# FFN output product: six of eleven pairs of feature tiles by seven products, in two passes over the columns

## The chip, the cores and the metric

The kernel runs on one core of a Trainium2 chip. The metric is the device time of one execution, in microseconds (us). TensorE (PE) multiplies 128x128 tiles: a weight load (PEld) puts the standing operand in place, and a matmul moves the other operand past it into a bank of PSUM. VectorE (DVE), ScalarE (ACT) and GpSimd (POOL) work on SBUF and PSUM, each through its own queue in order. SyncE (SP) issues most of the transfers.

## The reference, cut to what matters

One decoder layer for 512 tokens of width 1024: two mixers on a normalised input, an output projection, and a SwiGLU feed-forward part (FFN), each with a norm before and behind and a residual. The change touches the last product, the norm behind it and the residual:

```
def swiglu(hn, w_ffn_in, w_ffn_out):          # w_ffn_out: 2816 x 1024
    a, b = jnp.split(hn @ w_ffn_in, 2, axis=-1)
    return (jax.nn.silu(a) * b) @ w_ffn_out
...
    ff = swiglu(rmsnorm(h, norm_ffn_pre[l]), w_ffn_in[l], w_ffn_out[l])
    h = h + rmsnorm(ff, norm_ffn_post[l])
```

All inputs and the output are float32.

## The kernel before

Every product in float32 is made of three matmuls on operands split in two: `split` (L103) copies a tile to a high part (float32r) on ACT and has DVE subtract it from its source for the low part (`lo_of`, L100). High by high, high by low and low by high are summed in PSUM. So each operand costs one ACT copy and one DVE subtraction, both inputs of which lie in SBUF when the source does.

Many products go by Strassen's and Winograd's scheme: an operand is cut in four quarters, seven products of quarters and of their sums (`PRODUCTS`, L213: a for weights, s for their sums, b for tokens, t for theirs) take the place of eight. The sums of weights are made on POOL (L230, L258), the results are put together by DVE from PSUM (`seven`, L263).

The FFN's first product (L1268 to L1283) takes eleven pairs f2 of feature tiles. Each loads 256 columns for the gate and for the other half (`feat_quarters`, L221), runs `feat_seven` (L287) twice, seven products of 12 matmuls with 256 columns each, and leaves silu(a) * b in `gt` (L1283), which holds for each pair four quarters: two feature tiles by two halves of the tokens.

The second product, up to the end, is the stage in question. `rows` (L1300) loads two feature tiles of `w_ffn_out` (each 128 x 1024), splits them into `wh` and `wl`, and splits the gate tiles into `gh` and `gl` (`gate_split`, L1264). `product(i, c, f)` (L1314) makes three matmuls of 512 columns for token tile i, column half c and feature tile f, with the gate as the standing operand. Eight banks of PSUM hold all of the result (4 token tiles x 2 halves). The first 18 feature tiles go one after the other over all eight banks. The last four go bank by bank (L1330), so that a token tile is finished while others still run: sum of squares on ACT (L1337), gain on DVE (L1342), power on POOL (L1341), scaling and residual on DVE (L1346), output on SP's or ACT's queue (L1347).

What sets the order: raw weights come by SP's queue into a ring of four buffers (`wraw`, L80), split ones lie in a ring of five (`wun`, L81), each released when its reader is done. Within an engine a planner orders the instructions by a simulated timeline (L1387); where `pinned` is set (L1329) the matmuls stay in the program's order. Buffers of a pool that is closed are taken over by the next pool when their last readers are done.

Of the kernel before, what the change touches and what calls it, by code (L numbers as in the profile page):

```python
# [10 lines left out]
F32 = mybir.dt.float32  # L11
# [5 lines left out]
P = 128  # L17
# [17 lines left out]
def hybrid_block(  # L35
# [1224 lines left out]
    NPF, REST = NF // 2, 4  # L1260
    gt = gp.tile([P, NPF, 4, H], F32, name="gt")
    gs = {}

    def gate_split(f):  # L1264
        gs[f] = [gp.tile([P, T], F32R, tag=n, name=n, bufs=REST + 2) for n in ("gh", "gl")]
        split(*gs[f], gt[:, f // 2, 2 * (f % 2) : 2 * (f % 2) + 2, :].rearrange("p t n -> p (t n)"))

    with tc.tile_pool(name="s7", bufs=2, side=RS, reuse_waits="tile") as s7:  # L1268
        for f2 in range(NPF):
# [13 lines left out]
            nc.vector.tensor_tensor(gt[:, f2], qb, qa, op=ALU.mult)  # L1283
    s6c.close()
    ps_ac.close()
    ps_c = ctx.enter_context(tc.tile_pool(name="ps_c", bufs=4, space=PSUM))


    def bank_c():
        return ps_c.tile([P, 512], F32, tag="c", name="pc")  # L1290

    with tc.tile_pool(name="s8", bufs=2, side=RS, reuse_waits="tile") as s8:
        gfin = s8.tile([P, D], F32, name="gfin", bufs=1)
        nc.scalar.dma_start(gfin, g_ffn_post.to_broadcast([P, D]))
        banks = [(f(), f()) for f in (bank_p, bank_b, bank_c, bank_c)]

        def col(name):
            return s8.tile([P, 1], F32, tag=name, name=name, bufs=NT)

        def rows(f2):  # L1300

            raws = [raw_of(w_ffn_out[f * P : (f + 1) * P, :]) for f in (2 * f2, 2 * f2 + 1)]
            res = []
            for e in range(2):
                gate_split(2 * f2 + e)
                wh = wun.tile([P, D], F32R, tag="wh", name="wh")
                wl = wun.tile([P, D], F32R, tag="wl", name="wl")
                split(wh, wl, raws[e][:, 0, :])
                res.append((wh, wl))
            return res  # L1310

        ws = {}

        def product(i, c, f):  # L1314
            ts_, cs, dst = slice(i * P, (i + 1) * P), slice(512 * c, 512 * (c + 1)), banks[i][c]
            (wh, wl), (gh, gl) = ws[f], gs[f]
            mm(dst, gh[:, ts_], wh[:, cs], start=(f == 0), stop=False)
            mm(dst, gh[:, ts_], wl[:, cs], start=False, stop=False)
            mm(dst, gl[:, ts_], wh[:, cs], start=False, stop=(f == NF - 1))

        for f2 in range(NPF):
            ws[2 * f2], ws[2 * f2 + 1] = rows(f2)
            for f in (2 * f2, 2 * f2 + 1):
                if f < NF - REST:
                    for i in range(NT):
                        for c in range(2):
# [64 lines left out]
```

## Time and profile before

| | |
|---|---|
| median of three runs | 1178.73 us (1178.39 to 1178.78) |
| profiled execution | 1178.72 us, its span 1176.9 us |
| PE busy | 1164.9 us, 99% |
| DVE busy | 844.0 us, 72% |
| ACT busy | 532.1 us, 45% |
| POOL busy | 333.5 us, 28% |
| granted clock of TensorE | 0.999 |

The span runs from the first to the last instruction. Busy is the time in which an engine executes something, including time in which an instruction that has begun is held up. A row of a group reads: line, engine, operation, output <- inputs, shape, count, busy time, mean of one in ns, and the idle time before them with what ended it.

### The profile page before, as it was taken

How to read it: one execution, taken by the hardware profiler on the slowest of the kernel's cores; microseconds unless marked ns; L12 is line 12 of the kernel's file. 1: busy time of each engine (PE TensorE's matmuls, PEld its weight loads, DVE VectorE, ACT ScalarE, POOL GpSimd, SP SyncE). 2: the span in 40 equal slices, each digit the busy share in tenths (PEclk: the TensorE clock that was granted, in tenths of full speed). 3: DMA queues.
4: the chain of work that ended last, by engine and by line, in shares of the span. 5: the costliest groups of instructions: out<-in, count | busy, mean ns of one | idle time of the engine just before them, and what ended most of it. 6: DMA issues, size and time to landing. Idle time of an engine off the chain costs nothing.

```text
span 1176.9 us, 18856 instructions
## 1 busy us (share of the span) xinstructions
PE 1164.9 (99%) x7529; PEld 1056.3 (90%) x7529; DVE 844.0 (72%) x1120; ACT 532.1 (45%) x899; POOL 333.5 (28%) x358
## 2 busy tenths in 40 slices
PE   9999999999999999999999999999999999999997
PEld 7988999988899998998899898888999999998886
DVE  7488888888577873786586567767799998773333
ACT  6476666666233434434243334335455444442321
POOL 2021112126644403320240200001356676610000
PEclk9999999999999999999999999999999999999999
DMA  7332122222641323115122434344033333353311
GB/s 235 99 99 74 62 72 64 77 77 92 194 148 60 93 90 114 55 53 154 36 82 82 133 90 134 126 160 126 19 108 108 109 108 108 108 162 101 97 36 72
DMA packets 146536, 118.25 MB, mean 100 GB/s; under 512 B 3832, under 2 KB 135168, under 8 KB 146448
## 3 DMA queue, kind: packets, MB, share of 16 engines
q1 hardware_dynamic: 145856, 115.85, 32.5%
q8 instruction: 59, 0.97, 0.4%
q10 hardware_dynamic: 592, 1.20, 0.3%
q14 instruction: 29, 0.24, 0.1%
HBM read 109.96 MB, written 7.08 MB: 99 GB/s over the span
## 4 chain that ended last, share of the span: by engine, by line
PE 92%; DVE 5%; issue 1%; ACT 1%; DMA 0%; POOL 0%; POOLq 0%; DVEq 0%; ACTq 0%
PE pp L95 41%; PE pb L95 20%; PE pa L95 20%; PE pc L95 5%; PE px L95 3%; PE pb L98 3%; DVE wl L101 1%; DVE sm L603 1%; ACT wh L104 1%; DVE sl L101 0%; DMA ysb<-in_x_dram 0%; DVE al L101 0%; DVE kl L101 0%; DVE qb L101 0%; DVE qa L101 0%
## 5 line engine op out<-in xcount | busy, mean ns | idle before, releaser
L101 DVE TENSOR_TENSOR wl<-raw,wh 128x1024 fp32r<-128x1024 f32 x196 | 260.7, 1338 | 60.3 <-ACT wh L104 59.3
L104 ACT ACTIVATE wh<-raw 128x1024 fp32r<-128x1024 f32 x194 | 195.2, 1014 | 203.4 <-PE pa L95 59.5
L95 PE MATMUL pp<-hT,wh 128*128 128x512 f32 (+1 forms) x304 | 112.0, 369 | 0.0
L95 PE MATMUL pp<-hL,wh 128*128 128x512 f32 (+1 forms) x304 | 107.7, 354 | 0.0
L95 PE MATMUL pp<-hT,wl 128*128 128x512 f32 (+1 forms) x304 | 107.6, 354 | 0.0
L258 POOL TENSOR_TENSOR st<-raw 128x512 f32<-128x512 f32 x28 | 44.4, 1608 | 170.3 <-DMA raw<-in_w_in_dram 170.3
L101 DVE TENSOR_TENSOR wl<-st,wh 128x1024 fp32r<-128x1024 f32 x54 | 75.1, 1392 | 13.1 <-ACT wh L104 12.1
L95 PE MATMUL pp<-qk,wh 128*128 128x512 f32 x256 | 80.1, 394 | 0.0
L230 POOL TENSOR_TENSOR st<-raw 128x512 f32<-128x512 f32 x40 | 61.1, 1528 | 50.3 <-DVE wl L101 50.3
L95 PE MATMUL pp<-wh,hT 128*128 128x256 f32 (+1 forms) x240 | 73.9, 309 | 0.1
L95 PE MATMUL pp<-wl,hT 128*128 128x256 f32 (+1 forms) x240 | 73.0, 305 | 0.7 <-DVE wl L101 0.4
L95 PE MATMUL pp<-wh,hL 128*128 128x256 f32 (+1 forms) x240 | 73.0, 305 | 0.2 <-DVE hL L101 0.2
L104 ACT ACTIVATE wh<-st 128x1024 fp32r<-128x1024 f32 x54 | 56.6, 1056 | 35.6 <-PE pp L95 15.6
L95 PE MATMUL pa<-hL,wh 128*128 128x264 f32 (+1 forms) x208 | 66.2, 318 | 0.0
L95 PE MATMUL pa<-hT,wh 128*128 128x264 f32 (+1 forms) x208 | 66.2, 318 | 0.0
L95 PE MATMUL pa<-hT,wl 128*128 128x264 f32 (+1 forms) x208 | 66.1, 318 | 0.0
L603 DVE TENSOR_TENSOR_SCAN sm<-sm,mask 128x528 f32<-128x528 f32 (+1 forms) x64 | 54.8, 857 | 14.3 <-ACT sm L600 13.5
L95 PEld LDWEIGHTS pp<-hT,wl 128*128 128x128 f32 x304 | 57.2, 188 | 8.4
L613 POOL CAST mg<-sp 128x32 fp32r<-128x32 f32 x32 | 7.5, 233 | 197.6 <-DVE sp L604 153.7
L95 PEld LDWEIGHTS pp<-hT,wh 128*128 128x128 f32 x304 | 57.3, 188 | 5.8
L95 PEld LDWEIGHTS pp<-hL,wh 128*128 128x128 f32 x304 | 57.4, 189 | 5.3
L95 PEld LDWEIGHTS pp<-qk,wh 128*128 128x128 f32 x256 | 47.7, 188 | 10.7
(346 smaller groups left out, 3680.3 us busy)
## 6 DMA issues: line engine op xcount, KB each, us to landing
raw<-in_w_in_dram SPq DMA_DIRECT2D x88, 512.0 KB, 4.2
raw<-in_w_ffn_in_dram SPq DMA_DIRECT2D x44, 512.0 KB, 3.8
raw<-in_w_ffn_out_dram SPq DMA_DIRECT2D x22, 512.0 KB, 3.6
raw<-in_w_ret_out_dram SPq DMA_DIRECT2D x16, 512.0 KB, 3.4
raw<-in_w_sb_out_dram SPq DMA_DIRECT2D x8, 512.0 KB, 3.9
raw<-in_w_out_dram SPq DMA_DIRECT2D x8, 512.0 KB, 4.0
ysb<-in_x_dram SPq DMA_DIRECT2D x4, 512.0 KB, 7.1
gb_d<-go SPq DMA_DIRECT2D x8, 256.0 KB, 2.0
```

The source lines that it names most:

```text
L95: return keep(nc.tensor.matmul(*args, **kw))
L98: return keep(nc.tensor.transpose(dst, src, idn))
L101: return nc.vector.tensor_tensor(lo, src, hi.bitcast(F32), op=ALU.subtract)
L104: ins = nc.scalar.activation(hi, src, AF.Copy)
L230: ins = nc.gpsimd.tensor_tensor(d, p, q, op=op)
L258: nc.gpsimd.tensor_tensor(d[:, k : k + 2], p[:, k : k + 2], q[:, k : k + 2], op=op)
L603: nc.vector.tensor_tensor_scan(rev, rev, mask[:, r0:][:, ::-1], 0.0, op0=ALU.mult, op1=ALU.max)
L613: nc.gpsimd.tensor_copy(g[:, two, 0:NM], m)
```

## The change

The stage now runs in two passes g over the columns (512 each), and a step takes a pair f2 of feature tiles (256 features) with the 512 columns and all 512 tokens. Pairs with an even number go by seven products of quarters (42 matmuls of 256 columns), those with an odd number by plain products (24 of 512 columns). `prepare(n)` loads the weights of step n, has POOL make the sums of weights and tokens, and splits all. Split operands lie in four rooms of 16 KB, two of which are the buffers `th` and `tl` of the stage before. The second pass takes the pairs from 10 down; the first four find their operands still in the rooms and prepare only weights. Seven products and the plain ones share eight banks (`new_banks`; plain products go to the banks of a12 with a22, and of s4 with x22, a quarter of its own). `combine` puts them together at the end of each pass, in SBUF (`ys`). The first two steps are prepared within the stage before. The steps 19 (pair 1, plain), 20 and 21 (pairs 2 and 0) of the second pass are interleaved product by product, so that token tiles 2 and 3 are finished behind s4 and 0 and 1 behind the last product. The norm's gain of the first pass runs during the second; the gains of tiles 2 and 3 in the second, and one residual sum for tiles 0, 2 and 3, go to POOL.

```diff
@@ -1257,13 +1257,55 @@
     gp = ctx.enter_context(tc.tile_pool(name="gp", bufs=1, side=LS, reuse_waits="tile"))
-    NPF, REST = NF // 2, 4
+    NPF, REST = NF // 2, 2
     gt = gp.tile([P, NPF, 4, H], F32, name="gt")
-    gs = {}
-
-    def gate_split(f):
-        gs[f] = [gp.tile([P, T], F32R, tag=n, name=n, bufs=REST + 2) for n in ("gh", "gl")]
-        split(*gs[f], gt[:, f // 2, 2 * (f % 2) : 2 * (f % 2) + 2, :].rearrange("p t n -> p (t n)"))
+    ops, ws = {}, {}
+    plain = lambda f2: f2 % 2 == 1
+    def pair_of(n):
+        return n if n < NPF else (10, 9, 8, 7, 6, 5, 4, 3, 1, 2, 0)[n - NPF]
+    rooms4 = [(gp, "go"), (tn, "th"), (tn, "tl")]
+    def prepare(n, sums):
+        g, f2 = n // NPF, pair_of(n)
+        raw = raw_of(w_ffn_out[2 * P * f2 : 2 * P * (f2 + 1), 512 * g : 512 * (g + 1)])
+        A11, A21 = raw[:, 0, 0:256], raw[:, 0, 256:512]
+        A12, A22 = raw[:, 1, 0:256], raw[:, 1, 256:512]
+        seven_, kept = not plain(f2), g == 1 and f2 >= NPF - 4
+        if seven_:
+            w = sums.tile([P, 4, H], F32, tag="st", name="st")[:, 0:3, :]
+            S2, S3, S4 = w[:, 0, :], w[:, 1, :], w[:, 2, :]
+            todo = [(gt[:, f2, 1, :], gt[:, f2, 1, :], gt[:, f2, 0, :], ALU.subtract)] if g == 0 else []
+            todo += [(S3, A11, A21, ALU.subtract), (A21, A21, A22, ALU.add), (S2, A21, A11, ALU.subtract), (S4, A12, S2, ALU.subtract)]
+            if not kept:
+                t = sums.tile([P, 4, H], F32, tag="st", name="st")[:, 0:3, :]
+                T2, T3, T4 = t[:, 0, :], t[:, 1, :], t[:, 2, :]
+                B11, T1, B21, B22 = [gt[:, f2, q, :] for q in range(4)]
+                todo += [(T2, B22, T1, ALU.subtract), (T3, T2, B11, ALU.subtract), (T4, B21, T2, ALU.subtract)]
+            for d, p, q, op in todo:
+                nc.gpsimd.tensor_tensor(d, p, q, op=op)
+        wh, wl = wun_split(raw.rearrange("p k (c n) -> p (k c) n", c=2))
+        ws[n] = {k: (wh[:, v], wl[:, v]) for k, v in dict(a11=0, s1=1, a12=2, a22=3).items()}
+        ws[n]["rows"] = [[v[:, 2 * k : 2 * k + 2].rearrange("p c n -> p (c n)") for v in (wh, wl)] for k in range(2)]
+        if kept:
+            ops[n] = ops[pair_of(n)]
+        else:
+            place, name = rooms4[pair_of(n) % 4]
+            if g:
+                place, name = rooms4[(2, 1, 0, 3)[(n - NPF) % 4]]
+            o = place.tile([P, 4, KH, H], F32R, name=name, bufs=1).rearrange("p a b n -> p (a b) n")
+            split(o[:, 0:4], o[:, 8:12], gt[:, f2])
+            ops[n] = {k: (o[:, v], o[:, 8 + v]) for k, v in dict(b11=0, t1=1, b12=1, b21=2, b22=3, t2=4, t3=5, t4=6).items()}
+        if seven_:
+            wh, wl = wun_split(w)
+            ws[n].update({k: (wh[:, v], wl[:, v]) for k, v in dict(s2=0, s3=1, s4=2).items()})
+            if not kept:
+                split(o[:, 4:7], o[:, 12:15], t)
     with tc.tile_pool(name="s7", bufs=2, side=RS, reuse_waits="tile") as s7:
         for f2 in range(NPF):
@@ -1281,70 +1323,175 @@
             nc.scalar.activation(qa, qa, AF.Silu)
             feat_seven(ub_, ntok, qb)
             nc.vector.tensor_tensor(gt[:, f2], qb, qa, op=ALU.mult)
+        for n in range(2):
+            prepare(n, sst)
     s6c.close()
-    ps_ac.close()
-    ps_c = ctx.enter_context(tc.tile_pool(name="ps_c", bufs=4, space=PSUM))
-
-
-    def bank_c():
-        return ps_c.tile([P, 512], F32, tag="c", name="pc")
     with tc.tile_pool(name="s8", bufs=2, side=RS, reuse_waits="tile") as s8:
         gfin = s8.tile([P, D], F32, name="gfin", bufs=1)
         nc.scalar.dma_start(gfin, g_ffn_post.to_broadcast([P, D]))
-        banks = [(f(), f()) for f in (bank_p, bank_b, bank_c, bank_c)]
-
...
-                            product(i, c, f)
+        rooms4.append((s8, "o4"))
+        sc = [[s8.tile([P, 1], F32, tag=f"sc{i}{c}", name="sc", bufs=1) for c in range(2 + 2 * (i < 2))] for i in range(NT)]
+        ys = [s8.tile([P, 4, 512], F32, name="y", bufs=2) for _ in range(2)]
+        names = ["a11", "s2", "s1", "s3", "s4", "a12", "a22"]
+        pairs = dict(PRODUCTS)
+        both_of, single, banks, keys, begun = {}, {}, {}, {}, set()
+        def new_banks():
+            begun.clear()
+            for a, room in zip(names, (bank_p, bank_p, bank_b, bank_b)):
+                v = room()
+                banks[a], keys[a], single[a] = [v[:, 0:256], v[:, 256:512]], [a, a], v
+            for t, two in enumerate((("a12", "a22"), ("s4", "x22"))):
+                both_of[t] = bank_a()
+                for c, a in enumerate(two):
+                    banks[a], keys[a] = [both_of[t][:, s, 256 * c : 256 * (c + 1)] for s in range(2)], [(t, 0), (t, 1)]
+            both_of["a12"], both_of["a22"] = [both_of[0][:, :, 256 * c : 256 * (c + 1)] for c in range(2)]
+            both_of["s4"], both_of["x22"] = [both_of[1][:, :, 256 * c : 256 * (c + 1)] for c in range(2)]
+        def three(d, key, x, w):
+            mm(d, x[0], w[0], start=key not in begun, stop=False, skip_group_check=True)
+            begun.add(key)
+            mm(d, x[0], w[1], start=False, stop=False, skip_group_check=True)
+            mm(d, x[1], w[0], start=False, stop=True, skip_group_check=True)
+        def tile_of(n, b, s):
+            return [v[:, P * s : P * (s + 1)] for v in ops[n][b]]
+        def product(n, a, parts=(0, 1)):
+            for s in parts:
+                three(banks[a][s], keys[a][s], tile_of(n, pairs[a], s), ws[n][a])
+        def plain_products(n, tokens_=(0, 1)):
+            for t in tokens_:
+                for s in range(2):
+                    for k in range(2):
+                        three(both_of[t][:, s, :], (t, s), tile_of(n, f"b{k + 1}{t + 1}", s), ws[n]["rows"][k])
+        def step(n):
+            if plain(pair_of(n)):
+                plain_products(n)
+            else:
+                for a in names:
+                    product(n, a)
+        def add(d, p, q):
+            nc.vector.tensor_tensor(d, p, q, op=ALU.add)
+        def whole(a):
+            return single[a].rearrange("p (s n) -> p s n", s=2)
+        def combine(y, a):
+            q11, q21, q12, q22 = [y[:, q, :].rearrange("p (s n) -> p s n", s=2) for q in range(4)]
+            p = both_of[a] if a in both_of else whole(a)
+            if a == "x22":
+                nc.scalar.activation(q22, p, AF.Copy)
+            elif a == "a11":
+                nc.scalar.activation(q11, p, AF.Copy)
+            elif a == "s2":
+                add(q21, p, q11)
+            elif a == "s1":
+                add(q12, p, q21)
+                add(q22, q12, q22)
+            elif a == "s3":
+                add(q22, p, q22)
+                add(q21, p, q21)
+            elif a == "s4":
+                add(q12, p, q12)
+            elif a == "a12":
+                add(q11, p, q11)
+            else:
+                add(q21, p, q21)
+        def columns(y, i, g, cn):
+            n0, n1, s = cn.start, cn.stop, i % 2
+            return y[:, 2 * (i // 2) + n0 : 2 * (i // 2) + n1, 256 * s : 256 * (s + 1)], gfin[:, 512 * g + 256 * n0 : 512 * g + 256 * n1].rearrange("p (c n) -> p c n", n=256)
+        def squares(i, g, cn, dst):
+            v, _ = columns(ys[g], i, g, cn)
+            sq = s8.tile([P, 2, 256], F32, tag="sq", name="sq")[:, : cn.stop - cn.start, :]
+            nc.scalar.activation(sq, v, AF.Square, scale=D**-0.5, accum_out=dst)
+        def scaled(i, g, cn):
+            v, w = columns(ys[g], i, g, cn)
+            (nc.gpsimd if g and i > 1 else nc.vector).tensor_tensor(v, v, w, op=ALU.mult)
+        both = slice(0, 2)
+        def finish(i, n):
+            rs = s8.tile([P, 1], F32, tag="rs", name="rs", bufs=NT)
+            nc.vector.scalar_tensor_tensor(rs, sc[i][0], 1e-6, sc[i][n - 1], op0=ALU.add, op1=ALU.add)
+            nc.gpsimd.tensor_tensor(rs, rs, nhalf, op=ALU.pow)
+            for g in range(2):
+                v, _ = columns(ys[g], i, g, both)
+                cs = slice(512 * g, 512 * (g + 1))
+                h = h2[:, i, cs].rearrange("p (c n) -> p c n", c=2)
+                if g or i == 1:
+                    nc.vector.scalar_tensor_tensor(v, v, rs, h, op0=ALU.mult, op1=ALU.add)
+                else:
+                    nc.scalar.activation(v, v, AF.Copy, scale=rs)
+                    nc.gpsimd.tensor_tensor(v, v, h, op=ALU.add)
+                queue = nc.scalar if i == 1 and g else nc.sync
+                queue.dma_start(out[i * P : (i + 1) * P, cs].rearrange("p (c n) -> p c n", c=2), v)
+        order = ["x22"] + names
+        new_banks()
+        last = 2 * NPF - REST - 1
+        for n in range(last):
+            if n >= 2:
+                prepare(n, s8)
+            if n == NPF:
+                for a in order:
+                    combine(ys[0], a)
+                new_banks()
+            if NPF + 2 <= n < NPF + 2 + NT:
+                squares(n - NPF - 2, 0, both, sc[n - NPF - 2][0])
+                scaled(n - NPF - 2, 0, both)
+            step(n)
+        for n in range(last, 2 * NPF):
+            prepare(n, s8)
         pinned[0] = True
-        for i in range(NT):
-            sc, fo = [col("sc0"), col("sc1")], s8.tile([P, D], F32, tag="fo", name="fo")
...
-                queue.dma_start(out[i * P : (i + 1) * P, cs], fo[:, cs])
+        plain_products(last, (1,))
+        for a in names:
+            if a == "a22":
+                plain_products(last, (0,))
+                combine(ys[1], "a12")
+                combine(ys[1], "a22")
+            for parts in ((0, 1),) if a != "a22" else ((0,), (1,)):
+                if a == "a22":
+                    i = parts[0]
+                    banks[a][i], keys[a][i] = bank_p()[:, 0:256], ("last", i)
+                for n in range(last + 1, 2 * NPF):
+                    product(n, a, parts)
+                if a == "a22":
+                    cs = slice(256 * i, 256 * (i + 1))
+                    add(ys[1][:, 1, cs], banks[a][i], ys[1][:, 1, cs])
+                    if i == 0:
+                        for e in range(2):
+                            squares(e, 1, slice(0, 1), sc[e][1])
+                            scaled(e, 1, slice(0, 1))
+                            nc.gpsimd.tensor_tensor(sc[e][0], sc[e][0], sc[e][1], op=ALU.add)
+                    squares(i, 1, slice(1, 2), sc[i][2])
+                    scaled(i, 1, slice(1, 2))
+                    finish(i, 3)
+            if a == "a11":
+                combine(ys[1], "x22")
+            if a[0] == "s" or a == "a11":
+                combine(ys[1], a)
+            if a == "s4":
+                for i in (2, 3):
+                    squares(i, 1, both, sc[i][1])
+                    scaled(i, 1, both)
+                for i in (2, 3):
+                    finish(i, 2)
 # ---- launch: one core; inputs and outputs as the reference has them ----
```

More of the change, by code (lines that the diff above doesn't have):

```diff
@@ L1312, in hybrid_block @@
[L1312 to L1324, printed above, removed]
-                    for i in range(NT):
-                        for c in range(2):
-                            product(i, c, f)
```

27 lines of the change are left out of this document (removed).

## The prediction

> **What bounds the kernel now.** I read the page's span and engine shares first, then the table of stretches for the last 200 us, then the chain of waits, and last the single instructions at the places that the change touches.
>
> ```profile
> span 1176.9 us, 18856 instructions
> PE 1164.9 (99%) x7529; PEld 1056.3 (90%) x7529; DVE 844.0 (72%) x1120; ACT 532.1 (45%) x899; POOL 333.5 (28%) x358
> ```
>
> ```profile
> 972.00:1012.00 40.00, 40.00 (x338) 40.00 (x337) 33.30 (x35) 18.47 (x22) 26.28 (x17) 1.00 0.36 106
> 1041.00:1051.00 10.00, 10.00 (x86) 10.00 (x85) 6.31 (x8) 5.45 (x6) 0.00 (x0) 1.00 0.61 178
> 1051.00:1111.00 60.00, 60.00 (x267) 49.65 (x266) 22.96 (x24) 17.16 (x22) 0.00 (x0) 1.00 0.37 120
> 1111.00:1150.00 39.00, 39.00 (x174) 32.30 (x173) 12.74 (x13) 10.28 (x13) 0.00 (x0) 1.00 0.13 41
> ```
>
> The columns of the second are the stretch, its length, busy time and count of PE, PEld, DVE, ACT and POOL, the granted clock, and the DMA. PE has no idle time from 972 to 1150 and runs at full clock; in the stage to be changed (from 1051 on) DVE is busy 38% and less, and POOL not at all. So time leaves this stage only with matmul time, and DVE and POOL have room for additions, unless these get in each other's way. The chain of waits gives the pitch of matmuls (start, length, count):
>
> ```profile
> 1038.17 2.85 PE pb L95 x24
> ...
> 1048.19 2.85 PE pb L95 x24
> ...
> 1064.67 2.72 PE pc L95 x12
> 1070.11 2.72 PE pc L95 x12
> ```
>
> The first two rows are one group of seven products apart: 84 matmuls of 256 columns in 10.02 us, 119.3 ns each. The last two are 24 matmuls of 512 columns apart: 5.44 us, 226.7 ns each. Two narrow ones so cost 12 ns more than a wide one.
>
> **The change, part 1: the matmuls.** Before: 22 feature tiles x 4 token tiles x 2 column halves x 3 = 528 wide matmuls, 528 x 0.2267 = 119.7 us. After: per pass six pairs by 7 products x 2 halves x 3 = 42 narrow ones, and five pairs by 24 wide ones; over two passes 504 narrow and 240 wide. 504 x 0.1193 + 240 x 0.2267 = 60.1 + 54.4 = 114.5 us. **Removed: 5.2 us.** In the new narrow ones the tokens stand and the weights move, the other way round than in the rows above. The rows by tile show both ways in this kernel:
>
> ```profile
> L95 PE MATMUL pa<-wh,th x128: 277/283/364, 339.1 to 711.3; 128*128 128x256 f32 x128
> ...
> L95 PE MATMUL pa<-th,wh x80: 283/283/283, 856.2 to 1047.7; 128*128 128x256 f32 x80
> ```
>
> Their median is 283 ns either way, so I keep the pitch; at 24 in 2.85 us (118.8 ns) the gain is 5.4 us, at 120 ns 4.8 us.
>
> The Trainium skill (TensorE: Matmul & The Clock Gate, Back-to-back issue gap) gives N / 2.4 + 2.5 ns between warm matmuls; by that the gain would be 528 x 215.8 - 504 x 109.2 - 240 x 215.8 = 7.1 us. The rows above have 11 ns more on both widths, and decide.
>
> **Part 2: what DVE and POOL get.** A seven-product pair needs sums of weights and of tokens on POOL (8 operations of 128x256 in the first pass, 7 in the second, 4 where operands are kept), and then four DVE subtractions: two of 1024 columns, two of 768. A plain pair needs two of 1024. Their durations, from groups of the last stage, from all of POOL, and from the seven-product stage:
>
> ```profile
> L101 DVE TENSOR_TENSOR wl<-raw,wh 128x1024 fp32r<-128x1024 f32 x22 | 26.9, 1225 | 11.5 <-ACT wh L104 11.5
> ...
> L101 DVE TENSOR_TENSOR gl<-gt,gh 128x512 fp32r<-128x512 f32 x16 | 11.1, 694 | 51.2 <-ACT gh L104 51.2
> ```
>
> ```profile
> L196 POOL TENSOR_TENSOR ts<-hT x8: 732/748/1602, 275.7 to 320.1; 128x256 f32<-128x256 f32 x8
> ```
>
> The POOL row has 748 ns as its median and 1602 at most, and the reason is the point of this change. In the timeline of DVE, and in that of POOL, at two places:
>
> ```profile
> 317.33 1.44 DVE L101 TENSOR_TENSOR wl<-raw,wh 128x1024 fp32r<-128x1024 f32 x1 [0.53 <-ACT wh L104]
> ```
>
> ```profile
> 316.95 0.74 POOL L196 TENSOR_TENSOR ts<-hT 128x256 f32<-128x256 f32 x1 [1.69 <-DVE tl L101]
> 317.65 1.72 POOL L196 TENSOR_TENSOR tu<-hL 128x256 f32<-128x256 f32 x1
> ```
>
> ```profile
> 1011.73 1.48 DVE L1283 TENSOR_TENSOR gt<-ub 128x1024 f32<-128x1024 f32 x1
> 1013.13 2.31 DVE L101 TENSOR_TENSOR wl<-raw,wh 128x1024 fp32r<-128x1024 f32 x1
> ```
>
> ```profile
> 1012.08 2.29 POOL L230 TENSOR_TENSOR st<-raw,st 128x512 f32<-128x512 f32 x1
> ```
>
> ```profile
> L230 POOL TENSOR_TENSOR st<-st,raw 128x512 f32<-128x512 f32 x20 | 26.2, 1311 | 25.8 <-issue 25.7
> ```
>
> A DVE subtraction whose two inputs are both in SBUF and a POOL operation don't run together: they take turns. At 317 the DVE one ends at 318.77, so it truly ran from 317.55 (less 1.22); the second POOL one ends at 319.37, so it truly ran from 318.63 (less 0.74). In turns, then, 1024 DVE columns cost 318.63 - 317.55 = 1.08 us and 256 POOL columns 317.55 - 316.95 = 0.60 us; the rest of each duration hides behind the other engine. Without a DVE operation between them two POOL starts are 317.65 - 316.95 = 0.70 us apart. At 1012 gt, POOL and wl fill 1011.73 to 1015.44, 3.71 us, nearly the sum of 1.22, 1.31 (the group row) and 1.22.
>
> So I keep one account for both engines. DVE: 40 subtractions of 1024 (22 weights, 18 operands, as four are kept) x 1.08 = 43.2; 22 of 768 x 0.81 (scaled) = 17.8; five of 512 outside the end (four gains, one sum; 0.69 alone) x 0.6 = 3.0; the last gt 1.1. POOL: 6 x 8 + 2 x 4 + 4 x 7 = 84 operations; at 0.60 that is 50.4. Sum 115.5 us. Some of it is done before the stage begins at 1050.9, because the seven-product stage runs out of such work early:
>
> ```profile
> 1032.12 2.28 POOL L230 TENSOR_TENSOR st<-raw,st 128x512 f32<-128x512 f32 x1
> ```
>
> ```profile
> 1037.82 1.23 DVE L101 TENSOR_TENSOR wl<-st,wh 128x1024 fp32r<-128x1024 f32 x1
> 1038.96 0.68 DVE L280 TENSOR_TENSOR ub<-pa,ub 128x512 f32<-128x512 f32 x1
> 1040.23 0.69 DVE L101 TENSOR_TENSOR wl<-raw,wh 128x512 fp32r<-128x512 f32 x1 [0.58 <-ACT wh L104]
> ```
>
> POOL ends at 1034.4, DVE's subtractions for that stage at 1040.9. All of pair 0 (8 x 0.60 + 3.78 = 8.6), pair 1's weights (1.1) and three POOL operations of pair 2 (1.8) fit there: 11.5. Left are 104.0 us. The last operand is that of pair 0 for its second product in the last steps; behind that point PE has 10.6 us of matmuls (0.72 + 4 x 1.43 + 2.72 + 1.43), so it is due at 114.5 - 10.6 = 103.9. The account is **full to the brim**: short by 0.1 if every POOL operation falls between two DVE ones, and by 104.0 + 73 x 0.10 - 103.9 = 7.4 if none does (84 less the 11 done ahead). There are 67 DVE operations for 84, so 17 have no partner: 17 x 0.10 + 0.1 = **1.8 us of PE waiting**, my value; 0 to 7.4 its bounds. The seven-product stage speaks for the low half: in 20.04 us it has seven DVE operations of 1024 (six weights, one gt), two of 512 and eight POOL operations of 512 (1.31 less the same 0.14), 7.6 + 1.1 + 9.4 = 18.1 us, 90%, and PE has no idle time there.
>
> The Trainium skill (SBUF — State Buffer, Who interferes with whom) says that the port pair which DVE and GpSimd share is locked for a full instruction. Taken to the letter this is a rival, below; the traces agree on the turns, but 0.12 us of each instruction overlaps.
>
> Costed at nothing: ACT's copies (22 + 18 of 1024, 22 of 768, at about 1.05 and 0.8 us: 60 of 114 us); the weight loads, the same bytes in rows of 2 KB instead of 4; and the **turn of the passes**. There eight DVE additions of 512 columns, nearly all from PSUM (0.68 in the row at 1038.96; 0.6 apart, less the 0.08 by which wl at 1013.13 starts before gt is done) empty the banks. They start behind the second product of the last pair of the first pass, 3.6 us before its end, and the last bank is written again 3.6 us into the next step: 5.0 us of work in 7.2. Two subtractions queued ahead are hidden too; beyond that each costs PE 1.1 us.
>
> **Part 3: the end.** Before, behind the last matmul:
>
> ```profile
> 1170.36 0.39 PE L95 MATMUL pc<-wh,gl 128*128 128x512 f32 x1
> 1170.85 0.60 ACT L1337 ACTIVATE sq<-pc 128x512 f32<-128x512 f32 x1 [2.03 <-PE pc L95]
> 1171.34 0.20 ACT L1337 ACTIVATION_READ_ACCUMULATOR sq<-pc 128x1 f32 x1
> 1171.57 0.16 DVE L1340 SCALAR_TENSOR_TENSOR rs<-sc,sc 128x1 f32<-128x1 f32 x1 [2.03 <-ACT sq L1337]
> 1171.65 0.69 DVE L1342 TENSOR_TENSOR fo<-pc,gfin 128x512 f32<-128x512 f32 x1
> 1171.81 0.55 POOL L1341 TENSOR_TENSOR rs<-rs,nhalf 128x1 f32<-128x1 f32 x1 [4.89 <-DVE rs L1340]
> 1172.39 1.54 DVE L1346 SCALAR_TENSOR_TENSOR fo<-fo,rs,h 128x512 f32<-128x512 f32 x3
> ```
>
> From the moment the product can be read (1170.85) to the end of the span are 6.05 us: 3.08 to the last DVE result (1173.93), 2.97 for the output transfer. After, two token tiles end together instead of one. From 1.43 us before that moment, when the last plain products are done, DVE has: two additions of 512 (0.62 each), two of 256 and four gains of 256 (0.35 each, from the 425 ns below), two sums for the norms (0.1), three scalings of 512 for tiles 0 and 1 (0.68, the last 0.75), and two more for tiles 2 and 3 that wait for POOL: 1.24 + 0.70 + 1.40 + 0.20 + 2.11 + 1.36 = 7.0 us.
>
> ```profile
> L1346 DVE SCALAR_TENSOR_TENSOR fo<-fo,rs,h 128x512 f32<-128x512 f32 x7 | 5.0, 748 | 0.3
> ...
> L277 DVE TENSOR_TENSOR ub<-pp,ub 128x256 f32<-128x256 f32 x1 | 0.4, 425 | 0.1
> ```
>
> It is done 7.0 - 1.43 = 5.6 us behind the moment, with the transfer 8.55: **2.5 us more than before**. Low bound: tiles 2 and 3 are out of the way and only the dependent steps count (addition at 0.2, square to 1.1, power to 1.85, three scalings to 3.9, transfer): 0.8 more. High bound: POOL, in order, stands in front. It has for tiles 2 and 3 two gains and two sums of 512 (1.31 us each) and two powers (0.55), 6.3 us from 4.9 before the moment (5.58 us of matmuls lie behind the product that they need, less an addition), then two small sums and two powers, 2.2 us; where turns with DVE stretch it by 2 us, the last power is at 5.6, the end at 10.1: 4.0 more.
>
> **Sum**, against the profiled execution's 1178.72 us (its span 1176.9 and 1.8 around it, with a median of 1178.73): 1178.72 - 5.2 + 1.8 + 2.5 = **1177.8 us**, 0.9 less, which is no change that can be told (0.2% is 2.4 us, about what a measurement of this kernel resolves).
>
> **The rivals.**
> 1. *The gain comes through.* No waiting and a short end: 1178.72 - 5.2 + 0.8 = 1174.3; with half the extra end 1175.2. For it: the seven-product stage, with turns at 90%, lets PE wait nowhere, and four kept pairs make the start of the second pass light. Against it: in the first pass the turns ask for 6 x 8.6 + 5 x 2.2 = 62.6 us per 57.3 of PE, carried only by the head start.
> 2. *The turns of DVE and POOL become the bound (slower).* Place: the pairs 4 to 10 of the first pass and the last two of the second. With POOL operations back to back and 7.4 us of waiting: 1178.72 - 5.2 + 7.4 + 2.5 = 1183.4. It decides from 0.67 us per POOL operation on (73 x 0.07 + 0.1 = 5.2 of waiting: 2.5 us over). For it: the brim-full account, sums that depend on each other, and 'st' tiles that POOL gets back only behind DVE. Against it: DVE has an operation waiting nearly always when it is late. With whole durations, 84 x 0.74 + 40 x 1.22 + 22 x 0.92 + 4.7 = 135.9 us less 13.6 done ahead, PE waits 18.4 and the time is 1194.4. The skill's page named above would have it so.
> 3. *The turn of the passes holds PE.* With four subtractions ahead of the additions instead of two: 2.2 us more, 1180.0, and with a late end 1181.5. Against it: the next pairs there reuse operands and bring few.
>
> That fewer products are computed than said can't be: their count stands in the code.
>
> **How the numbers follow.** Forecast 0.40 (its own range 1176.4 to 1181.0, waiting and end together 2.9 to 7.5). Rival 1: 0.36, all faster by over 0.2%. Rival 2: 0.20, of it 0.03 for whole durations. Rival 3: 0.04, counted slower. So faster 0.36, same 0.40, slower 0.24. The range goes from 1174.0 (rival 1 with the 5.4 us gain, 1174.1) to 1185.0 (rival 2 with a late end); above lie whole durations and rival 2 with both bounds.
>
> **What would show it.** 504 narrow and 240 wide matmuls at 119 and 227 ns show part 1. Part 2: idle time of PE or its loads put down to ACT or DVE on 'wh', 'go', 'th', 'tl', 'o4', above all in the first pass behind its fourth pair; a POOL operation of 256 columns whose mean is 1 us and more, beside DVE subtractions over 1.5 us. None of this and PE full to the end is rival 1. Part 3: the time from the last matmul to the end, 6.5 us now, about 9 by me. The prediction is wrong if PE waits at the start of the stage, where I see pair 0 ready in time, or if the narrow matmuls keep another pitch.

## The result, and the profile after

The changed kernel takes 1188.80 us (median of four runs, 1187.44 to 1189.02), the kernel before beside it 1178.76 (1178.39 to 1178.86): a ratio of 1.0083 with an interval of 1.0066 to 1.0101. It is **slower by about 10 us**, 3.8 us above the top of the predicted range.

The head of the page, after:

```profile
span 1186.8 us, 19467 instructions
PE 1164.3 (98%) x7745; PEld 1066.0 (90%) x7745; DVE 895.7 (75%) x1152; ACT 559.7 (47%) x928; POOL 444.5 (37%) x449
```

The table of stretches for the stage, after; columns as in the prediction:

```profile
1050.00:1062.00 12.00, 12.00 (x81) 11.04 (x80) 11.18 (x8) 5.92 (x6) 9.96 (x8) 1.00 0.26 87
1062.00:1066.00 4.00, 3.04 (x23) 2.63 (x23) 2.50 (x4) 3.35 (x4) 3.02 (x4) 1.00 0.41 131
1066.00:1105.00 39.00, 39.00 (x241) 35.17 (x240) 28.67 (x22) 17.44 (x20) 32.98 (x27) 1.00 0.36 109
...
1110.00:1114.00 4.00, 1.68 (x11) 1.47 (x12) 3.90 (x4) 2.33 (x4) 3.76 (x4) 0.98 0.47 140
1114.00:1121.00 7.00, 6.18 (x28) 5.78 (x27) 6.18 (x9) 1.47 (x2) 4.42 (x7) 0.52 0.31 102
...
1125.00:1162.00 37.00, 37.00 (x224) 33.17 (x224) 28.07 (x21) 18.60 (x21) 27.57 (x21) 1.00 0.17 54
1162.00:1166.00 4.00, 3.05 (x23) 2.65 (x22) 2.15 (x3) 2.49 (x4) 0.61 (x1) 1.00 0.00 0
```

PE is full for most of the stage and loses time at three places: step 2 (the second seven-product pair, 1062 to 1066), the turn of the passes (1110 to 1121), and step 21 (the last pair, 1162 to 1166). Narrow matmuls at 119.3 ns would fill 4 us with 33; the first and the last of these stretches hold 23. At the turn the granted clock is 0.52 for 7 us on top of the waiting.

The span grew by 9.9 us, and the starts of the matmuls give its parts. The stage begins 0.3 earlier (1050.59 for 1050.9). Its 504 narrow and 240 wide matmuls need 5.2 less. From its first matmul to its last, PE loses 10.2 us against that pitch: counted gap by gap 1.5 at step 2, 6.8 at the turn, 1.5 at step 21, and 0.4 scattered. From the end of the last matmul (its start and one pitch) to the end of the span are 11.47 us for 6.34, 5.13 more. With two decimals: -0.29 - 5.16 + 10.21 + 5.13 = 9.89.

The chain of waits, after, runs through POOL where before it had nothing but PE:

```profile
1054.48 1.68 POOL raw L1291
1056.15 5.05 POOL st L1291 x3
...
1065.01 3.39 POOL st L1291 x3
...
1072.67 1.40 POOL st L1291
...
1083.43 1.40 POOL st L1291
...
1093.19 1.40 POOL st L1291
...
1102.70 1.91 issue
1104.65 1.38 POOL st L1291
1106.87 1.07 ACT wh L104
1107.96 1.46 DVE wl L101
```

The starts at 1072.67, 1083.43, 1093.19 and 1104.65 are the first sums of one seven-product pair each: 10.8, 9.8 and 11.5 us apart. PE takes 10.45 us for two steps, one of seven products and one plain (42 x 0.1193 + 24 x 0.2267). So over the first two periods the chain of sums is as slow as PE and gains no lead: PE comes to these pairs 10.9, 10.6 and 11.4 us after their first sums. The third period spans a single step of PE, 5.0 us, because steps 10 and 11 are both seven-product steps; PE is at step 11 only 5.1 us after its first sum (1109.78). Here the chain falls behind.

The groups of the stage, after (1050 to the end):

```profile
L101 DVE TENSOR_TENSOR wl<-raw,wh 128x1024 fp32r<-128x1024 f32 x20 | 32.3, 1619 | 7.7 <-ACT wh L104 7.5
L1291 POOL TENSOR_TENSOR st<-raw 128x256 f32<-128x256 f32 x22 | 29.2, 1328 | 23.5 <-DVE tl L101 12.1 <-PE pb L95 5.3 <-DVE go L101 3.8
...
L1291 POOL TENSOR_TENSOR raw<-raw 128x256 f32<-128x256 f32 x11 | 15.2, 1379 | 0.8
...
L1291 POOL TENSOR_TENSOR st<-st,gt 128x256 f32<-128x256 f32 x9 | 12.5, 1392 | 0.1
```

The same subtraction took 1225 ns before; a POOL operation that takes 0.74 us alone takes 1.33 to 1.39 on average. The last numbers of the second row, POOL's idle time, matter as much. The view of waits takes the 12.1 us apart (total, number, longest):

```profile
POOL st L1291 <- DVE tl L101: 12.1, 3, 8.9
```

The longest, 8.9 us, is in the second pass (1122.0 to 1130.9), ahead of the sums for its last pairs. In the first pass POOL stood idle for 1.25, 1.25, 1.25 and 1.95 us right before the four starts above, 5.7 us in all, until DVE had done a `go` or a `tl`, because the two tiles of the ring `st` were still in use. So the engine that was late was also made to wait.

The turn of the passes, from the timeline, after (start, length, engine):

```profile
1104.65 1.37 POOL L1291 TENSOR_TENSOR st<-raw 128x256 f32<-128x256 f32 x1 [1.95 <-DVE tl L101]
...
1106.87 1.06 ACT L104 ACTIVATE wh<-raw 128x1024 fp32r<-128x1024 f32 x1 [2.56 <-POOL raw L1291]
...
1107.96 1.59 DVE L101 TENSOR_TENSOR wl<-raw,wh 128x1024 fp32r<-128x1024 f32 x1 [2.53 <-ACT wh L104]
...
1109.48 1.48 DVE L101 TENSOR_TENSOR wl<-st,wh 128x768 fp32r<-128x768 f32 x1
...
1110.21 0.57 ACT L1395 ACTIVATE y<-pp 128x512 f32<-128x512 f32 x1
...
1110.89 1.75 DVE L101 TENSOR_TENSOR wl<-raw,wh 128x1024 fp32r<-128x1024 f32 x1
...
1112.57 0.68 DVE L1383 TENSOR_TENSOR y<-pp,y 128x512 f32<-128x512 f32 x1
```

POOL's sums for step 11 can start only at 1104.65. ACT and DVE, each in order, stand behind them: ACT's copy that empties the bank of a11 (L1395) and DVE's first addition (L1383) come after the preparations, at 1110.21 and 1112.57. PE had its last product of a11 in the first pass done between 1105 and 1106; the next fills wait for the bank:

```profile
1110.84 0.38 PE L95 MATMUL pp<-wh,tl 128*128 128x256 f32 x1 [0.90 <-ACT y L1395]
...
1113.30 0.39 PE L95 MATMUL pp<-wh,tl 128*128 128x256 f32 x1 [1.48 <-DVE y L1383]
...
1117.23 0.55 PE L95 MATMUL pb<-wh,tl 128*128 128x256 f32 x1 [0.82 <-DVE y L1383]
```

The three gaps are 1.06, 1.64 and 1.11 us beyond the pitch. Of the other 3.0 of the 6.8 us, 2.6 are the slow clock: narrow matmuls start 0.21 us apart for 0.12. The last 0.4 are four matmuls at full clock that start 0.10 us late each, two of them right behind a gap.

The end, from DVE's timeline, after:

```profile
1173.28 1.78 DVE L1436 SCALAR_TENSOR_TENSOR y<-y,rs,h 128x512 f32<-128x512 f32 x1 [0.53 <-POOL rs L1430]
1174.98 1.28 DVE L1383 TENSOR_TENSOR y<-pa,y 128x512 f32<-128x512 f32 x2
1176.18 1.08 DVE L1436 SCALAR_TENSOR_TENSOR y<-y,rs,h 128x512 f32<-128x512 f32 x1
...
1180.32 3.08 DVE L1436 SCALAR_TENSOR_TENSOR y<-y,rs,h 128x512 f32<-128x512 f32 x3 [0.37 <-POOL rs L1430]
```

DVE begins its first two additions for tiles 0 and 1 at 1174.98, behind a scaling of 1.78 us, and has its last result at 1183.40; the transfer takes 3.4 us. Scalings average 1222 ns here for 748 before, as POOL's gains and residual sums run beside them.

### The profile page after: what moved, and what is told of

Same layout as the page of the kernel before. It is cut to its first block, busy times and chain, and to the rows that moved or that the text cites. A ratio compares the mean times of both kernels' runs of the same rounds, so it can differ in the third digit from the quotient of the medians.

```text
span 1186.8 us, 19467 instructions
## 1 busy us (share of the span) xinstructions
PE 1164.3 (98%) x7745; PEld 1066.0 (90%) x7745; DVE 895.7 (75%) x1152; ACT 559.7 (47%) x928; POOL 444.5 (37%) x449
## 3 DMA queue, kind: packets, MB, share of 16 engines
q10 hardware_dynamic: 720, 1.33, 0.3%
## 4 chain that ended last, share of the span: by engine, by line
PE 84%; DVE 7%; POOL 6%; issue 2%; ACT 1%; DVEq 0%; POOLq 0%
PE pp L95 38%; PE pa L95 21%; PE pb L95 18%; POOL st L1291 4%; PE px L95 3%; PE pb L98 3%; DVE wl L101 2%; POOL raw L1291 1%; DVE sm L603 1%; ACT wh L104 1%; DVE y L1383 1%; DVE al L101 0%; DVE y L1436 0%; PE pp L760 0%; DVE sp L604 0%
## 5 line engine op out<-in xcount | busy, mean ns | idle before, releaser
L101 DVE TENSOR_TENSOR wl<-raw,wh 128x1024 fp32r<-128x1024 f32 x196 | 265.9, 1365 | 57.4 <-ACT wh L104 56.1
L101 DVE TENSOR_TENSOR wl<-st,wh 128x1024 fp32r<-128x1024 f32 (+1 forms) x66 | 86.4, 1309 | 18.1 <-ACT wh L104 17.0
L104 ACT ACTIVATE wh<-st 128x1024 fp32r<-128x1024 f32 (+1 forms) x66 | 67.2, 1018 | 54.0 <-PE pp L95 30.5
L95 PE MATMUL pa<-wh,th 128*128 128x256 f32 (+1 forms) x216 | 64.0, 324 | 0.0
```

Of the source, the lines that this page charges most:

```text
L95: return keep(nc.tensor.matmul(*args, **kw))
L101: return nc.vector.tensor_tensor(lo, src, hi.bitcast(F32), op=ALU.subtract)
L104: ins = nc.scalar.activation(hi, src, AF.Copy)
```

## The experiments

What had to be told apart: whether PE waits because DVE and POOL have too much to do, because their turns stretch each step of a dependent chain, or because of the ring or the turn of the passes; and how much of the loss is the end alone. Each kernel is the changed one with one edit. PE's loss is counted gap by gap, without the 0.3 to 0.7 us that are scattered in every run; counted so, the changed kernel loses 9.8 us.

**1. No sums.**

```diff
-            for d, p, q, op in todo:
-                nc.gpsimd.tensor_tensor(d, p, q, op=op)
+            w = raw.rearrange("p k (c n) -> p (k c) n", c=2)[:, 0:3]
+            t = gt[:, f2, 0:3]
```

> Leaves out all sums of weights and of tokens that POOL makes for the seven products; the splits take unsummed quarters of the same size in their place, so DVE, ACT and PE have the same instructions as in the changed kernel. Theory (DVE's subtractions and POOL's sums take turns, and this is what makes PE wait): the mean of a DVE subtraction of 1024 columns in the stage falls from about 1.65 to 1.22-1.3 us, PE loses under 1.5 us between the start of the stage and its last matmul instead of 10.2, and the time is 1178 to 1180.5 us, the end being as long as in the changed kernel. Rival (the order of the queues at the turn of the passes: additions that empty the banks stand behind preparations, whoever makes the sums): the waits near 1062 and 1163 go, those of the turn (about 6.7 us with the slow clock behind them) stay, time about 1185.5.

1179.37 us (1178.75 to 1179.98), ratio to before 1.0007 [0.9997, 1.0017]. PE waits nowhere in the stage: from its first matmul to the end of its last are 115.1 us, for 114.5 computed. A row of its groups:

```profile
L101 DVE TENSOR_TENSOR wl<-raw,wh 128x1024 fp32r<-128x1024 f32 x21 | 25.5, 1222 | 20.9 <-ACT wh L104 20.8
```

With the POOL operations gone the subtraction is back at 1222 ns, and all of PE's loss goes with them. What is left above before is the long end, and a stage that begins 0.9 us later (1051.76).

**2. The same sums on DVE.**

```diff
-                nc.gpsimd.tensor_tensor(d, p, q, op=op)
+                nc.vector.tensor_tensor(d, p, q, op=op)
```

> The 84 sums of 256 columns go from POOL to DVE; nothing else. Theory (turns): a sum costs 0.35 us on DVE (0.42 alone, less the overlap) where it costs 0.60 to 0.70 in turns, so the common account falls from 115.5 to 94.5 us; PE loses under 2.5 us, time 1178.5 to 1181. Rival (DVE has too much to do as it is, with or without POOL): 29 us more on DVE make PE wait longer than now, time 1192 or more.

1179.88 us (1179.26 to 1180.22), ratio 1.0010 [1.0001, 1.0020]; PE loses 0.6 us. Groups and a stretch:

```profile
L1291 DVE TENSOR_TENSOR st<-raw 128x256 f32<-128x256 f32 x22 | 9.0, 417 | 0.0
```

```profile
1051.00:1080.00 29.00, 28.79 (x187) 26.15 (x186) 28.30 (x42) 18.55 (x20) 0.00 (x0) 1.00 0.35 108
```

All the sums are made, with the same dependencies and the same ring; only the engine differs. One takes 417 ns on DVE, and DVE with 98% in the first 29 us still keeps PE fed. So neither the sums as such, nor the ring by itself, nor DVE's amount of work makes PE wait. What no run separates is POOL's slower operation (0.74 us) from its stretching beside DVE, because no run has POOL's sums without the turns. An estimate from rows: seven of them 0.70 us apart would take 4.9 us for a pair, where 9.5 were measured (1072.67 to 1082.18), so that the turns make up most of what the chain has too much.

**3. The same POOL work, read by nobody.** POOL runs as many operations of the same size, from the same tiles, into a tile `un`; the splits take unsummed quarters.

```diff
-            w = sums.tile([P, 4, H], F32, tag="st", name="st")[:, 0:3, :]
...
+            u = s_un[0].tile([P, 4, H], F32, tag="un", name="un", bufs=1)
...
+            w = raw.rearrange("p k (c n) -> p (k c) n", c=2)[:, 0:3]
+            t = gt[:, f2, 0:3]
```

> POOL makes as many operations of the same size from the same tiles, but writes them to a tile that nobody reads; the splits take unsummed quarters, so the sums are left out of the result. Theory (turns between the engines): DVE's subtractions of 1024 columns stay slow, 1.5 us or more in the mean, but nothing waits for POOL any more, so PE loses 0 to 3 us and the time is 1178.5 to 1182. Rival (DVE isn't held by POOL; it only waits for late sums): the mean of a subtraction is 1.3 us or less.

1180.92 us (1179.96 to 1181.29), ratio 1.0018 [1.0008, 1.0028]; PE loses 1.25 us, at 1058 to 1060. Groups and a stretch:

```profile
L101 DVE TENSOR_TENSOR wl<-raw,wh 128x1024 fp32r<-128x1024 f32 x21 | 33.4, 1614 | 4.7 <-ACT wh L104 4.7
```

```profile
1061.00:1105.00 44.00, 44.00 (x270) 39.61 (x269) 41.15 (x26) 20.45 (x23) 43.45 (x31) 1.00 0.31 99
```

The turns are as heavy as in the changed kernel (1614 ns for 1619), both engines are 94% and 99% busy, and yet PE is full. So the work of both fits; 8.5 of the 9.8 us come only when somebody **reads** the sums. This run also takes the ring `st` away, which the next makes larger.

**4. A ring of four `st` tiles.**

```diff
-            w = sums.tile([P, 4, H], F32, tag="st", name="st")[:, 0:3, :]
+            w = sums.tile([P, 4, H], F32, tag="st", name="st", bufs=2 if n < 2 else 4)[:, 0:3, :]
...
-                t = sums.tile([P, 4, H], F32, tag="st", name="st")[:, 0:3, :]
+                t = sums.tile([P, 4, H], F32, tag="st", name="st", bufs=2 if n < 2 else 4)[:, 0:3, :]
```

> The sums' tiles in the stage get a ring of four instead of two. Theory (POOL is held by the ring: it gets a tile back only behind DVE, 12 + 4 us of waiting in the trace): POOL starts sums up to one pair earlier, PE loses 6 us or less instead of 10.2, time 1183 to 1185.5. Rival (the turns fill the time with or without the ring): time 1187 to 1189.5.

1185.43 us (1185.19 to 1185.68), ratio 1.0056 [1.0038, 1.0075]. PE loses 5.7 us. Stretches and POOL's timeline:

```profile
1062.00:1072.00 10.00, 6.37 (x37) 5.50 (x36) 7.80 (x6) 6.21 (x7) 7.90 (x8) 0.83 0.19 54
1072.00:1105.00 33.00, 33.00 (x210) 29.98 (x209) 28.39 (x20) 15.86 (x17) 32.61 (x25) 1.00 0.41 128
1105.00:1125.00 20.00, 20.00 (x138) 18.64 (x137) 15.51 (x18) 8.70 (x16) 14.03 (x15) 1.00 0.33 106
```

```profile
1064.57 1.41 POOL L1291 TENSOR_TENSOR st<-raw 128x256 f32<-128x256 f32 x2
1065.94 3.11 POOL L1291 TENSOR_TENSOR st<-raw,st 128x256 f32<-128x256 f32 x2
```

The losses at the turn and at step 21 are gone, and POOL no longer waits for a `tl` or a `go`. Step 2 became worse: with tiles free, the planner put sums of the next seven-product pair in front of the last one that step 2 waits for, and PE stood still for 3.6 us. This blurs the run: the first sum for step 11 now starts 5.4 us earlier (1099.21 for 1104.65), which is the ring, but PE also comes to step 11 4.7 us later (1114.50 for 1109.78), which is the wait at step 2. That the ring carried the lateness to the turn fits both and is not shown by itself.

**5. The turn first.** At step 11 the copy of a11 and the first addition go ahead of the preparations on ACT and DVE (an order-only dependence), and step 12's behind all additions.

```diff
-            if n >= 2:
-                prepare(n, s8)
...
+                if n == NPF:
+                    stand_behind(made[m0], turn[1])
+                    stand_behind(low[l0], turn[2])
+                if n == NPF + 1:
+                    stand_behind(made[m0], turn[1])
+                    stand_behind(low[l0], turn[-1])
```

> The changed kernel with another order at the turn of the passes only: the copy of a11's bank stands ahead of the weights of step 11 on ACT, the first addition ahead of their subtraction on DVE, and the weights of step 12 behind all additions. Theory (at the turn the additions are late because preparations stand in front of them in the queues): what PE loses between 1105 and 1125 falls from 6.7 us to 3-4.5, time 1185 to 1187. Rival (the sums of pair 10 themselves are late on POOL, whatever the order): the loss stays above 6 us, time 1188 to 1189.5.

1187.33 us (1186.72 to 1187.95), ratio 1.0072 [1.0054, 1.0091]. The turn still costs PE 4.1 us. The order of the queues is worth some 2.7 us of PE's time there, 1.1 of them because the slow clock lasted 3.4 us in place of 6.8; that the rest follows from late sums is argued, not shown. The time came out just above what was expected.

**6. Fewer seven-product pairs: four of eleven.**

```diff
-    plain = lambda f2: f2 % 2 == 1
+    plain = lambda f2: f2 not in (0, 2, 6, 10)
```

> Four of eleven pairs by seven products (0, 2, 6 and 10) instead of six, the others plain. PE gets 4 x 0.43 = 1.7 us more to do. Theory (turns): the account falls by 22 us, 82 us that are due after 105; PE loses 1 to 3 us, time 1181 to 1183. Rival (the turn of the passes alone): the 6.7 us there stay, time 1186 to 1187.5.

1181.69 us (1181.28 to 1182.73), ratio 1.0028 [1.0016, 1.0040]; PE loses 1.2 us, nearly all of it at step 2. With more plain steps between, the chain catches up, though steps 10 and 11 are still both of seven products. Here 1.7 us of matmul gain is given back, and the time is 7.1 us less.

**7. The end without POOL:** gains of tiles 2 and 3 and all scalings on DVE.

```diff
-            (nc.gpsimd if g and i > 1 else nc.vector).tensor_tensor(v, v, w, op=ALU.mult)
+            nc.vector.tensor_tensor(v, v, w, op=ALU.mult)
...
-                if g or i == 1:
+                if True:
```

> At the end alone: the gains of token tiles 2 and 3 and all scalings with residual go to DVE, so that POOL has only the powers and two small sums. Theory (in the end, too, POOL's operations hold DVE's): the scalings on DVE fall from 1.0-1.8 to 0.75 us, the stretch from the last matmul to the end of the span from 11.5 to 9-10 us, time 1186.5 to 1187.8. Rival (POOL's share is a relief for DVE): DVE has five operations of 512 columns more (3.3 us), the end is 12.5 us or more, time 1189.5 or more.

1188.07 us (1187.64 to 1188.72), ratio 1.0081 [1.0066, 1.0096]; the end takes 10.64 us for 11.47, less gain than expected.

```profile
L1436 DVE SCALAR_TENSOR_TENSOR y<-y,rs,h 128x512 f32<-128x512 f32 x8 | 5.5, 748 | 0.7 <-POOL rs L1430 0.7
```

The scalings are at 748 ns again, but there are eight for five, and two gains more. On balance POOL's share in the end costs 0.8 us of the 5.1. That the rest comes from two tiles that end together on one engine is what the next runs try.

**8. One token tile last, sums on DVE.** The second pass takes its seven-product pairs first; three plain pairs come last, token tile by token tile, with everything else already in `ys`, so that one addition from PSUM finishes a tile.

```diff
-    NPF, REST = NF // 2, 2
+    NPF, REST = NF // 2, 3
...
-        return n if n < NPF else (10, 9, 8, 7, 6, 5, 4, 3, 1, 2, 0)[n - NPF]
+        return n if n < NPF else (10, 9, 8, 7, 6, 4, 2, 0, 5, 3, 1)[n - NPF]
...
-                nc.gpsimd.tensor_tensor(d, p, q, op=op)
+                nc.vector.tensor_tensor(d, p, q, op=op)
...
+        for i in range(NT):
+            t, s = i // 2, i % 2
+            for n in range(last, 2 * NPF):
+                for k in range(2):
+                    three(both_of[t][:, s, :], (t, s), tile_of(n, f"b{k + 1}{t + 1}", s), ws[n]["rows"][k])
+            v, w = columns(ys[1], i, 1, both)
+            add(v, both_of[t][:, s, :].rearrange("p (c n) -> p c n", c=2), v)
```

> Sums on DVE as in the run before, and another end: the second pass takes pairs 10, 9, 8, 7, 6, 4, 2, 0 first, puts their products together in SBUF, and then runs the plain pairs 5, 3 and 1 token tile by token tile, so that one tile ends last, with one addition, square, gain, power and scalings on DVE. Theory: from the last matmul to the end 6.7 to 7.3 us instead of 11.4, PE loses 0.6 to 1.5 us, time 1174.6 to 1176.3, faster than both. Rival (DVE can't keep up with the pairs 6, 4, 2, 0 in a row, 6.2 us of DVE for 5.0 us of PE each): PE loses 4 us or more there, time 1178 to 1180.

1179.00 us (1178.59 to 1180.81), ratio 1.0003 [0.9994, 1.0012]: a miss. The end is down to 7.2 us (10.6 in number 7, which has no POOL work there either), but PE loses 3.3. The waits of PE's loads:

```profile
PEld pa L95 <- DVE y L1383: 2.4, 2, 1.2
```

Tiles 0 and 1 share a tile of PSUM, and so do 2 and 3: PE can't start the second of two while DVE reads the first, 1.05 us each time.

**9. The same, tiles in the order 0, 2, 1, 3.**

```diff
-        for i in range(NT):
+        for i in (0, 2, 1, 3):
```

> As the run with sums on DVE and the end tile by tile, but the token tiles in the order 0, 2, 1, 3. There PE waited twice for DVE's addition of the tile just done (0.94 us behind tile 0 and behind tile 2, with the loads), because tiles 0 and 1, and 2 and 3, lie in one tile of PSUM. Theory: with another PSUM tile in between these waits go, 2.1 us with the slow pitch behind them; time 1176.4 to 1177.4, faster than both kernels. Rival (PE waits for DVE as such): no change, 1178.5 to 1179.5.

**1176.35 us** (1176.02 to 1177.59, eleven runs), ratio 0.9981 [0.9972, 0.9990]: 2.25 us below before in the runs beside it (1178.60), and the only version that beats both kernels. PE loses 1.2 us, the end takes 7.2. The stage itself began at 1051.67, 1.1 us later than in the changed kernel. Over all profiles here this start lies between 1050.5 and 1052.0; why was not followed up.

**10. The same end with the sums on POOL:** number 9 without the edit of `nc.gpsimd`.

```diff
-                nc.vector.tensor_tensor(d, p, q, op=op)
+                nc.gpsimd.tensor_tensor(d, p, q, op=op)
```

> The same end, with the sums on POOL as in the changed kernel. Theory: the end is as short as with sums on DVE (7.4 us instead of 11.5), and PE loses at least the 8 us at the start and at the turn of the passes, more where four seven-product pairs follow one another; time 1184 to 1189. Rival (the longer end is itself due to POOL's late sums): the end stays above 10 us.

1187.07 us (1186.97 to 1187.17), ratio 1.0071 [1.0052, 1.0089]. The end takes 7.3 us, PE loses 11.1, again at step 2 and the turn, and at 1147 to 1159 where the pairs of seven now follow each other. End and chain are two separate losses.

## Why the prediction was wrong

**Part 1 was right.** The wide and the narrow matmuls kept their pitch (226.7 and 118.8 to 119.3 ns), and with no sums the stage took 115.1 us for 114.5. Pair 0 was ready, as predicted: PE did not wait at the start, but at step 2. Three small slips in the prediction change nothing: the overlap of the turns is 0.14 us by its own rows (1.22 - 1.08 and 0.74 - 0.60), not 0.12; the pitch is 10 to 11 ns above the formula, not 11 at both widths; and rival 2 with both bounds (1178.72 - 5.2 + 7.4 + 4.0 = 1184.9) lies within the range, not above it.

**Part 2 had the mechanism and not the sum.** The turns of DVE and POOL came as the two places of the trace before had shown: 1619 ns for 1225, POOL at 1.3 to 1.7 us, idle time put down to `wh` and `go`. The Trainium skill (SBUF — State Buffer, Who interferes with whom) says that a DVE instruction with two SBUF inputs contends with a GpSimd instruction that reads SBUF; the trace agrees, 1222 ns without POOL for 1619 with it. The rival with whole durations (1194.4) did not come.

The step that failed is "17 x 0.10 + 0.1 = 1.8 us of PE waiting". It pools the work of two engines and asks whether it is done by one due time near the end. Number 3 measures just that question: the same operations, read by nobody, cost PE 1.25 us, so the account was good for what it counted. But the sums are a chain: three POOL operations in a row (S2 needs the sum before it, S4 needs S2), then ACT's copy, then DVE's subtraction, and only then a free `st` tile for the next pair. Each POOL link that meets a DVE subtraction lasts about 1.7 us for 0.74, and while a link waits, its engine may have nothing else to do: POOL idled 5.7 us for `go` and `tl` before the sums of pairs 6, 8, 10 and step 11. Beside an account that is full there must be no such idle time. The seven-product stage, which I took as a sign for the low half, has work 90% full, but its sums are ready far ahead: the last ends at 1034.4, 16.5 us before that stage is over. The sign that the prediction named for part 2, POOL operations over 1 us beside subtractions over 1.5, was seen in number 3 as well and so does not tell whether PE waits.

My bound of 7.4 held only the case that no POOL operation falls between two DVE ones. Neither idle links nor what lateness does further on were in it, nor that two seven-product steps follow one another at the turn.

**The turn of the passes was costed at nothing, and cost 6.8 us.** The window of 7.2 us for 5.0 of additions was near as an amount: the first seven of eight took 5.1 us in a row (1112.57 to 1117.69). But rival 3 stood apart from rival 2, and they are one: the preparations in front of the additions were themselves waiting for POOL. In an in-order queue the additions then wait for sums that they don't need. "Beyond that each costs PE 1.1 us" was too little for the third subtraction, which held DVE from 1110.89 to 1112.57, and it left out the start of the first, 1107.96. Numbers 4 and 5 bear on this: with a larger ring (and a PE that comes later) the loss at the turn goes, with the queues' order alone a good third of it.

**The slow clock was in no term.** 2.6 us of the 6.8 are matmuls at a granted clock of 0.52.

**Part 3 had the right driver and too small a size:** 5.1 in place of 2.5, above its bound of 4.0. DVE's last result (1183.40) came 7.8 us behind the moment at which the last product can be read (1175.6), where I computed 5.6. Five scalings were priced at 0.68 to 0.75 and measured 1.22, as POOL's work beside them was thought of as a queue that might be late, not as one that takes turns with them; number 7 gives 0.8 us for it, net of the work that DVE takes over there. The transfer took 3.4 us for 2.97. The rest is DVE's queue: the first additions began 0.6 us ahead of that moment, not 1.43.

In the terms of the prediction: 1178.72 - 5.2 - 0.3 + 10.2 + 5.1 = 1188.5, against 1188.6 for the profiled execution. Rival 2 comes nearest: it named the turns, the sums that depend on each other and the `st` tiles that come back late, with 7.4 us of waiting for 10.2 and an end of 2.5 for 5.1. Its places were others, however: in pairs 4 to 10 of the first pass PE lost 0.2 us. Nor did its deciding point, 0.67 us per POOL operation in the common account, decide: number 3 has as many operations and turns just as heavy, and loses 1.25 us.

## What to carry to other kernels

Where one engine's results feed another, and both take turns at the same memory, don't compare sums of work with the time there is: follow one result through all its links, each with its stretched duration, to the buffer that it frees, and compare this period with the bound engine's. In a chain like this one, small sums that feed DVE belong on DVE: there a sum of 256 columns takes 417 ns and stretches nothing, on POOL it takes 0.74 to 1.7 us and stretches DVE's own instructions as well. At a turn of phases look at what stands in front of the work that frees the banks in each in-order queue, and let one tile, not two, end last.

## What the hardware showed that I had not expected

Two waits of PE of 1.06 and 1.64 us with some 0.7 us of matmuls between them (1109.8 to 1113.3) were enough: from 1114 on the granted clock is 0.52 for 7 us. Waits of 0.77 and 0.51 us at step 2, and of 0.36 and 1.01 us with one matmul between them at step 21, left it at 1.00. The Trainium skill (TensorE: Matmul & The Clock Gate, HAM oscillation — how this bites in real kernels) warns of idle gaps of more than about 3.4 us. By that none of these gaps would have slowed the clock; here it fell without any gap over 1.7 us, and what counts in this trace is nearer to the share of a stretch of that length in which PE works: of the 4 us from 1110, PE was busy for 1.68, of those from 1062 and from 1162 for 3.04 and 3.05. In number 4 a single gap of 3.6 us slowed it too (0.83 over 1062 to 1072). In number 10 PE was busy for 1.52 of the 3.4 us up to 1149.4, and the clock stayed at 1.00; so where the limit lies, and whether it matters where the stretch begins, stays open.
